# A fourth Strassen weight combination in a tile of its own, and four activation combinations moved between the products

## The chip, the cores and the metric

The kernel runs on one core of one Trainium2 chip. The metric is the device time of one execution in microseconds. A time is the median of several runs. The profile is one execution of its own, so it has its own time, and its trace has a span: the first to the last recorded instruction.

## The reference, cut to what matters

The model is one inference step through two layers. Each layer holds two SwiGLU feed-forward blocks ("FFN") around a token mixer, all in 32-bit floats. There are 640 token rows: 512 latent and 128 of context. Only the FFN matters here:

```python
def swiglu(h, w_in, w_out):
    a, b = jnp.split(h @ w_in, 2, axis=-1)
    return (jax.nn.silu(a) * b) @ w_out

n = rmsnorm(x, ng[0]) * (1.0 + mod[..., 1, :]) + mod[..., 0, :]
x = x + 0.5 * mod[..., 2, :] * swiglu(n, lp['w_ffn_in'][0], lp['w_ffn_out'][0])
```

`w_in` is 1024 x 5632 (two halves of 2816 columns, the a half and the b half) and `w_out` is 2816 x 1024.

## The kernel before

**Tiles and products.** Activations lie transposed: 128 channels by 320 tokens, two token halves (h = 0 and 1), eight blocks of channels. A product of 32-bit floats is made as three matmuls with a high and a low part each: hi x hi, hi x lo, lo x hi. So every weight block that arrives (a "raw" tile `wr_*`, 512 KB) is split: ScalarE (ACT) casts the high part (`wh_*`), VectorE (DVE) subtracts it from the raw block to get the low part (`wl_*`). The weights are read once; TensorE (PE) is the engine that has most to do.

**Quads.** Three of the four FFNs are "fast": layer 0's second (about 1262 to 1700 us of the trace), layer 1's first (1727 to 2150) and layer 1's second (2850 to 3300). In them 18 of the 22 column blocks of `w_in` are computed with a Strassen-Winograd 2x2 scheme, class `Quad`, 54 quads in all. A quad takes one a block `fa` and one b block `fb`, and needs seven products (`p` 1 to 7) of 12 matmuls each in place of the eight that plain blocks need. Its weights come in four groups:

- group 0: `wh_fa`, `wl_fa`, the a block itself (products 1 and 2). With it GpSimd (POOL) makes the combinations, four instructions that stand one behind the other: L86 `ws` (S1), L87 `ws` (S2), L88 S3 in place in `fb`, L89 S4 in place in the upper half of `fa`.
- group 1: `wh_g<-wr_fb`, `wl_g<-wr_fb` (products 7 and 4), split out of `fb` after L88.
- group 2: `wh_g<-ws`, `wl_g<-ws` (products 6 and 5).
- group 3: `whg` (L97) and `wlg` (L98), half a tile, split out of S4 (product 3).

PE takes the products of quad after quad in the order 1, 7, 3 of the quad before, 6, 4 of the quad before, 2, 5. Products 1, 6 and 5 accumulate in one PSUM tile `qx`, which ACT copies out after each of them (`qs`, L124) before PE may add the next; products 7 and 4 go to `qw`, product 2 to `qy`. After product 3 come ACT and DVE instructions that make the FFN's hidden values: `sa` (L1465, L1468), and their split `fhi`, `flo` (L903, L904).

**Queues and pools.** Each engine runs its own instruction list in order. SyncE (SP) issues the weight loads in order (L1235). Raw tiles come from a pool of three buffers (`RAW = 3`): a quad's two blocks and one of the next. `emit` walks the list of steps and asks for a load as soon as enough raw blocks count as "gone": a tuple says for each of a quad's four groups how many are let go with it, (0, 0, 1, 1) before. A load that reuses a buffer waits for the last instruction that reads or writes the block that was in it.

**Activation combinations.** Product 4 needs a combined activation, made by `combine4` in four chunks (k = 0 to 3): DVE adds `e` (L1404), POOL adds `t` (L1403) and subtracts `t - e` (L1405), ACT casts `nhi` and DVE makes `nlo` (L903, L904 through `put`). Tile `e` has tag "nt" with two buffers, which it shares with the copies `qs` of products 1 and 5; `t` has tag "tt", two buffers. An FFN is done in four parts of its hidden columns (5, 5, 6 and 6 blocks), q = 0 to 3. In part 0 the first four column blocks are plain (`pa`, `pb`), since the combinations are made meanwhile, so part 0 has a single quad; its products come in the order 1, 7, 6, 2, 5, 3, 4. `rest` issues all four `combine4` before that quad.

Of the kernel before, what the change touches and what calls it, by code (L numbers as in the profile page):

```python
# [10 lines left out]
F32 = mybir.dt.float32  # L11
# [6 lines left out]
P = 128  # L18
# [46 lines left out]
class Quad:  # L65
# [12 lines left out]
    def split(self, g, raws):  # L78
        b, sub, add = self.b, ALU.subtract, ALU.add
        fa, fb = raws  # L80
        T = b.nc.gpsimd.tensor_tensor
        if g == 0:
            self.s = b.tq.tile([P, 8, P], F32, tag="ws", name=f"ws_{self.name}", bufs=1)
            r = b.split(self.blocks[0], fa)
            s2, s1 = self.s[:, 0:4], self.s[:, 4:8]
            T(s1, fb[:, 0:4], fb[:, 4:8], add)  # L86
            T(s2, s1, fa[:, 0:4], sub)  # L87
            T(fb[:, 0:4], fa[:, 0:4], fb[:, 0:4], sub)  # L88
            T(fa[:, 4:8], fa[:, 4:8], s2, sub)  # L89
            return r  # L90
        if g == 1:
            return b.split((None, 8, f"g2{self.name}"), fb)
        if g == 2:
            return b.split((None, 8, f"g3{self.name}"), self.s)
        hi = b.tq.tile([P, 4, P], F32R, tag="whi4", name=f"whg4{self.name}", bufs=1)
        lo = b.tq.tile([P, 4, P], F32R, tag="wlo4", name=f"wlg4{self.name}", bufs=1)
        b.nc.scalar.copy(hi, fa[:, 4:8])  # L97
        b.nc.vector.tensor_tensor(lo, fa[:, 4:8], hi.bitcast(F32), sub)  # L98
        return hi, lo

    def product(self, out, w, p, first):
# [54 lines left out]
class Build:  # L156
# [1101 lines left out]
    def emit(self, steps):  # L1258


        last, order, seen = {}, [], set()
        for i, st in enumerate(steps):
            if not callable(st):
                last[id(st[0])] = i
                if id(st[0]) not in seen:
                    seen.add(id(st[0]))
                    order.append(st[0])

        blocks, splits = [], []
        done = {id(u): [] for u in order}  # L1270
        for u in order:
            n0 = len(blocks)
            if isinstance(u, Quad):
                blocks += u.blocks
                for g in range(4):
                    splits.append((u, lambda u=u, g=g, n0=n0: u.split(g, raws[n0 : n0 + 2]), n0 + 2, (0, 0, 1, 1)[g], g == 3))
            else:
                for i, tl in enumerate(u[0]):
                    blocks.append(tl)
                    splits.append((u, lambda tl=tl, n=n0 + i: self.split(tl, raws[n]), n0 + i + 1, 1, False))  # L1280
        raws = []
        cnt = {"split": 0, "gone": 0, "live": 0, "fourth": 0}

        def load():
            raws.append(self.load(blocks[len(raws)]))

        def room():
            return cnt["fourth"] < 1 if splits[cnt["split"]][4] else cnt["live"] < SPL

        def split():  # L1290
            u, f, need, gone, fourth = splits[cnt["split"]]
            while len(raws) < need:
                load()
            with self.ahead(WS):
                done[id(u)].append(f())
            cnt["split"] += 1
            cnt["gone"] += gone
            cnt["fourth" if fourth else "live"] += 1

        def fill():  # L1300
            while True:
                while len(raws) < len(blocks) and len(raws) - cnt["gone"] < RAW:
                    load()
                if cnt["split"] == len(splits) or not room():
                    break
                split()

        fill()
        for i, st in enumerate(steps):
            if callable(st):  # L1310
                st()
                continue
            u, h = st
            quad = isinstance(u, Quad)
            while len(done[id(u)]) < (u.NEED[h] if quad else len(u[0])):
                assert room()
                split()
            if quad:
                u.run(done[id(u)], h)
                cnt["live"] -= u.FREE[h]  # L1320
                cnt["fourth"] -= h == 3
                if u.FREE[h] or h == 3:
                    fill()
                if h in (6, 5):
                    self.late()
                    self.tick()
                continue
            with self.ahead(EV):
                u[1](done[id(u)], h)
            self.late()  # L1330
            self.tick()
            if last[id(u)] == i:
                cnt["live"] -= len(u[0])
                fill()
# [80 lines left out]
    def ffn(self, l, i, pre=None, post=None, fast=False, late=None):  # L1415
# [4 lines left out]
        steps = []  # L1420
        for q, nf in enumerate(FPARTS):
            j0 = sum(FPARTS[:q])
            end = q == len(FPARTS) - 1
            f = {}
# [13 lines left out]
            ins, outs, quads = [], [], []  # L1438
# [53 lines left out]
            if fast and q == 0:  # L1492

                def rest():
                    while self.deferred:
                        self.late()
                    for k in range(4):
                        self.combine4(k, f"{l}{i}")

                steps.append(rest)  # L1500
            steps += Quad.steps(quads)
            if end and late:
                steps.append(late)
            steps += self.edges(outs, 0, 4 if end else 0, post=post if end else None)
# [240 lines left out]
```

## Time and profile before

| | us |
|---|---|
| median of 3 runs | 3338.36 (3335.77 to 3343.9) |
| the profiled execution | 3330.81 |
| its span in the trace | 3329.0 |
| PE busy in it | 3213.5 (97%) |
| DVE busy | 2124.0 (64%) |
| ACT busy | 1291.7 (39%) |
| POOL busy | 494.8 (15%) |

The mean granted TensorE clock of the profiled execution is 0.989 of full speed. Times in the trace are counted from the span's start. A busy PE is a PE with a matmul in flight: it can be busy and still lose time between two matmuls, so the idle time of PE and of its weight loads (PEld) are both read below.

### The profile page before, as it was taken

To read this page: it belongs to the slowest core of one execution; us is meant where nothing else is said; L and a number is where in the kernel's file an instruction comes from. 1 tells how busy PE (TensorE), PEld (TensorE's weight loads), DVE (VectorE), ACT (ScalarE), POOL (GpSimd) and SP (SyncE) were. 2 spreads that over 40 slices of the span, in tenths; PEclk is the share of its full clock that TensorE was granted. 3 is DMA by queue.
4 is the path that set the end of the run, shared out by engine and by line. 5 is a ranking of instruction groups with operands and counts; after the bars stand their busy time and mean duration, and the time that the engine had idled before them with its cause. 6 is when DMAs were issued, how large, how long until landed. Compare 5 with 4: busy or idle time off the path is not lost.

```text
span 3329.0 us, 56455 instructions
## 1 busy us (share of the span) xinstructions
PE 3213.5 (97%) x22321; PEld 3028.1 (91%) x22321; DVE 2124.0 (64%) x4543; ACT 1291.7 (39%) x2596; POOL 494.8 (15%) x418
## 2 busy tenths in 40 slices
PE   6999999989999999999999999998999999999998
PEld 5887999879989999899998889997998999999998
DVE  5656574796686348566667556668758734856665
ACT  4233233554453224234343323445545423433432
POOL 0000000120000013222312312312000000322231
PEclk8999999989999999999999999998999999999999
DMA  6666433433313324522224553234331243122222
GB/s 220 185 192 205 129 117 109 131 113 98 92 50 115 92 73 120 173 83 83 75 80 145 175 160 89 67 117 122 98 90 52 63 138 88 53 75 79 87 70 76
DMA packets 493995, 364.55 MB, mean 110 GB/s; under 512 B 22466, under 2 KB 468260, under 8 KB 490916
## 3 DMA queue, kind: packets, MB, share of 16 engines
q1 hardware_dynamic: 463284, 311.33, 31.4%
q10 hardware_dynamic: 30448, 49.62, 4.3%
q8 instruction: 176, 2.88, 0.4%
q14 instruction: 87, 0.71, 0.1%
HBM read 327.33 MB, written 33.55 MB: 108 GB/s over the span
## 4 chain that ended last, share of the span: by engine, by line
PE 75%; DVE 15%; issue 4%; ACT 3%; DMA 3%; POOL 0%; DVEq 0%; ACTq 0%; SPq 0%; POOLq 0%
PE po L1254 6%; PE po L1255 6%; PE po L1256 6%; PE mg L1254 3%; PE mg L1256 3%; PE mg L1255 3%; PE qx L108 2%; PE qx L109 2%; PE pa L1254 2%; PE mps L284 2%; PE qx L110 2%; PE pa L1255 2%; PE pa L1256 2%; PE pb L1255 2%; PE pb L1254 2%
## 5 line engine op out<-in xcount | busy, mean ns | idle before, releaser
L1254 PE MATMUL po<-fhi,wh_fo 128*128 128x320 f32 x1408 | 444.6, 316 | 0.2
L1255 PE MATMUL po<-flo,wh_fo 128*128 128x320 f32 x1408 | 435.7, 310 | 0.0
L1256 PE MATMUL po<-fhi,wl_fo 128*128 128x320 f32 x1408 | 435.3, 310 | 0.0
L1254 PEld LDWEIGHTS po<-fhi,wh_fo 128*128 128x128 f32 x1408 | 263.9, 188 | 36.0 <-issue 31.5
L360 POOL TENSOR_TENSOR acc<-acc,sq 128x320 f32<-128x320 f32 x72 | 77.3, 1074 | 1339.2 <-ACT sq L359 1339.0
L1255 PEld LDWEIGHTS po<-flo,wh_fo 128*128 128x128 f32 x1408 | 264.5, 188 | 3.2 <-issue 2.7
L1256 PEld LDWEIGHTS po<-fhi,wl_fo 128*128 128x128 f32 x1408 | 264.2, 188 | 2.3 <-issue 2.3
L1254 PE MATMUL mg<-nhi,wh_wg 128*128 128x320 f32 x768 | 239.3, 312 | 0.0
L1256 PE MATMUL mg<-nhi,wl_wg 128*128 128x320 f32 x768 | 238.1, 310 | 0.0
L1255 PE MATMUL mg<-nlo,wh_wg 128*128 128x320 f32 x768 | 237.7, 310 | 0.0
L1244 ACT CAST wh_fo<-wr_fo 128x640 fp32r<-128x640 f32 (+1 forms) x128 | 100.0, 781 | 236.5 <-PE po L1255 183.9
L1510 DVE SCALAR_TENSOR_TENSOR xT0b<-po,mod,xT0b 128x64 f32<-128x64 f32 (+1 forms) x256 | 86.9, 379 | 149.6 <-PE po L1256 149.3
L1254 PE MATMUL pa<-nhi,wh_fa 128*128 128x320 f32 x544 | 173.2, 319 | 1.0 <-ACT nhi L422 1.0
L1255 PE MATMUL pa<-nlo,wh_fa 128*128 128x320 f32 x544 | 168.1, 312 | 1.2 <-DVE nlo L423 1.1
L1256 PE MATMUL pa<-nhi,wl_fa 128*128 128x320 f32 x544 | 168.5, 310 | 0.0
L1256 PE MATMUL pb<-nhi,wl_fb 128*128 128x320 f32 x544 | 168.4, 310 | 0.0
L1255 PE MATMUL pb<-nlo,wh_fb 128*128 128x320 f32 x544 | 168.3, 309 | 0.0
L1254 PE MATMUL pb<-nhi,wh_fb 128*128 128x320 f32 x544 | 168.2, 309 | 0.0
L86 POOL TENSOR_TENSOR ws<-wr_fb 128x512 f32<-128x512 f32 x54 | 73.9, 1368 | 624.5 <-DMA wr_fb<-in_w_ffn_in_dram 529.2
L1244 ACT CAST wh_fa<-wr_fa 128x1024 fp32r<-128x1024 f32 x88 | 92.5, 1051 | 149.0 <-PE po L1255 93.3
L1254 PEld LDWEIGHTS mg<-nhi,wh_wg 128*128 128x128 f32 x768 | 144.5, 188 | 2.3 <-issue 1.9
L1255 PEld LDWEIGHTS mg<-nlo,wh_wg 128*128 128x128 f32 x768 | 144.3, 188 | 0.5 <-issue 0.5
(531 smaller groups left out, 9818.7 us busy)
## 6 DMA issues: line engine op xcount, KB each, us to landing
wmod<-in_w_mod_dram SPq DMA_DIRECT2D x144, 512.0 KB, 4.1
wr_fa<-in_w_ffn_in_dram SPq DMA_DIRECT2D x88, 512.0 KB, 4.0
wr_fb<-in_w_ffn_in_dram SPq DMA_DIRECT2D x88, 512.0 KB, 4.5
wr_fo<-in_w_ffn_out_dram SPq DMA_DIRECT2D x64, 384.0 KB, 3.4
wr_wg<-in_w_in_dram SPq DMA_DIRECT2D x48, 512.0 KB, 4.4
wr_fo<-in_w_ffn_out_dram SPq DMA_DIRECT2D x64, 320.0 KB, 3.5
pqd<-s5pq ACTq DMA_DIRECT2D x16, 1024.0 KB, 7.6
wr_wb<-in_w_branch_dram SPq DMA_DIRECT2D x48, 256.0 KB, 2.8
```

Source lines behind the costliest of these rows:

```text
L86: T(s1, fb[:, 0:4], fb[:, 4:8], add)
L108: mm(out, a, ahi(k), start=(first and k == 0), stop=False, skip_group_check=True)
L109: mm(out, a, alo(k), start=False, stop=False, skip_group_check=True)
L110: mm(out, c, ahi(k), start=False, stop=(k == 3), skip_group_check=True)
L284: nc.tensor.matmul(pm[32 * j : 32 * j + 32, :256], self.sc[:, k, :], w[:, j * 256 : (j + 1) * 256], start=(k == 0), stop=(k == KD - 1),)
L360: (nc.vector if k == KD - 1 else nc.gpsimd).tensor_tensor(self.acc[:, h], self.acc[:, h], sq, ALU.add)
L1244: nc.scalar.copy(hi[:, :kk], raw[:, :kk])
L1254: nc.tensor.matmul(out, hi[:, k], ahi(k), start=(k == 0), stop=False)
L1255: nc.tensor.matmul(out, hi[:, k], alo(k), start=False, stop=False)
L1256: nc.tensor.matmul(out, lo[:, k], ahi(k), start=False, stop=(k == kk - 1))
L1510: self.nc.vector.scalar_tensor_tensor(x, po[:, sl], gate[:, n, g : g + 1], x, ALU.mult, ALU.add)
```

## The change

Three edits. S4 (L89) goes into a tile of its own, `ws4`, with one buffer, and `whg` and `wlg` are split out of that tile; nothing writes into `fa` any more. The tuple of raw blocks let go becomes (1, 1, 0, 0). And `combine4` leaves `rest`: its four chunks are put as steps of their own between the products of part 0's single quad: 1, chunk 0, 7, chunk 1, 6, chunk 2, 2, chunk 3, 5, 3, 4.

```diff
@@ -86,7 +86,8 @@
             T(s1, fb[:, 0:4], fb[:, 4:8], add)
             T(s2, s1, fa[:, 0:4], sub)
             T(fb[:, 0:4], fa[:, 0:4], fb[:, 0:4], sub)
-            T(fa[:, 4:8], fa[:, 4:8], s2, sub)
+            self.s4 = b.tq.tile([P, 4, P], F32, tag="ws4", name=f"ws4{self.name}", bufs=1)
+            T(self.s4, fa[:, 4:8], s2, sub)
             return r
@@ -94,8 +95,8 @@
         hi = b.tq.tile([P, 4, P], F32R, tag="whi4", name=f"whg4{self.name}", bufs=1)
         lo = b.tq.tile([P, 4, P], F32R, tag="wlo4", name=f"wlg4{self.name}", bufs=1)
-        b.nc.scalar.copy(hi, fa[:, 4:8])
-        b.nc.vector.tensor_tensor(lo, fa[:, 4:8], hi.bitcast(F32), sub)
+        b.nc.scalar.copy(hi, self.s4)
+        b.nc.vector.tensor_tensor(lo, self.s4, hi.bitcast(F32), sub)
         return hi, lo
@@ -1273,7 +1274,7 @@
                 for g in range(4):
-                    splits.append((u, lambda u=u, g=g, n0=n0: u.split(g, raws[n0 : n0 + 2]), n0 + 2, (0, 0, 1, 1)[g], g == 3))
+                    splits.append((u, lambda u=u, g=g, n0=n0: u.split(g, raws[n0 : n0 + 2]), n0 + 2, (1, 1, 0, 0)[g], g == 3))
@@ -1494,11 +1495,14 @@
                 def rest():
                     while self.deferred:
                         self.late()
-                    for k in range(4):
-                        self.combine4(k, f"{l}{i}")
 
                 steps.append(rest)
-            steps += Quad.steps(quads)
+            st = Quad.steps(quads)
+            if fast and q == 0:
+
+                for k in range(4):
+                    st.insert(2 * k + 1, lambda k=k: self.combine4(k, f"{l}{i}"))
+            steps += st
```

In the changed program lines behind L89 have moved by one: S4 is L90, `whg` and `wlg` are L98 and L99, `e` is L1405. The order of PE's instructions does not change at all.

What waits for what does change. Before, the load of the next quad's `fb` takes over a buffer that is free when DVE has made `wl_g<-wr_fb` of the current quad, and the load of the `fa` behind it one that is free at `wlg`, the last reader of the raw `fa`. After, the next `fb` takes the current `fa`'s buffer, which is free when DVE has made `wl_fa` and POOL has made S4; the `fa` behind it takes the current `fb`'s, free at `wl_g<-wr_fb`.

POOL's list in two quads of the second part, before (L86 to L89 are S1, S2, S3, S4; `wr_fa`, `wr_fb` the raw blocks):

```order
L86 TENSOR_TENSOR ws_14816<-wr_fb_14731 128x512
L87 TENSOR_TENSOR ws_14816<-ws_14816,wr_fa_14589 128x512
L88 TENSOR_TENSOR wr_fb_14731<-wr_fa_14589,wr_fb_14731 128x512
L89 TENSOR_TENSOR wr_fa_14589<-wr_fa_14589,ws_14816 128x512
L86 TENSOR_TENSOR ws_14949<-wr_fb_14864 128x512
```

and POOL's list at the same place with the change:

```order
L86 TENSOR_TENSOR ws_14819<-wr_fb_14651 128x512
L87 TENSOR_TENSOR ws_14819<-ws_14819,wr_fa_14537 128x512
L88 TENSOR_TENSOR wr_fb_14651<-wr_fa_14537,wr_fb_14651 128x512
L90 TENSOR_TENSOR ws_14827<-wr_fa_14537,ws_14819 128x512
L86 TENSOR_TENSOR ws_14953<-wr_fb_14829 128x512
```

The order is the same. But L89 overwrote the `fa` block that DVE's `wl_fa` still had to read, and so had to wait for it; L90 writes `ws4` (shown as `ws_14827`) and has nothing of DVE's to wait for but the `wlg` of the quad before.

ACT's list at the single quad of part 0 of the first fast FFN, before (`nhi` are the casts of the four chunks, the two `qs` the copies of `qx` after products 1 and 6):

```order
L1244 CAST wh_g_14007<-ws_13872 128x1024
L1451 ACTIVATE sa_13996<-pa_13946 128x320
L903 CAST nhi<-t_14025 128x320
L903 CAST nhi<-t_14032 128x320
L903 CAST nhi<-t_14039 128x320
L1244 CAST wh_fo_14019<-wr_fo_13712 128x640
L1453 CAST fhi_13328<-sa_13996 128x320
L903 CAST nhi<-t_14046 128x320
L124 COPY qs_14066<-qx_14053 128x320
L124 COPY qs_14093<-qx_14053 128x320
```

and with the change:

```order
L1245 CAST wh_g_14012<-ws_13872 128x1024
L1452 ACTIVATE sa_14001<-pa_13951 128x320
L1245 CAST wh_fo_14020<-wr_fo_13712 128x640
L1454 CAST fhi_13328<-sa_14001 128x320
L125 COPY qs_14039<-qx_14026 128x320
L904 CAST nhi<-t_14041 128x320
L904 CAST nhi<-t_14061 128x320
L904 CAST nhi<-t_14088 128x320
L904 CAST nhi<-t_14116 128x320
L125 COPY qs_14080<-qx_14026 128x320
```

The copy after product 1 has moved ahead of all four casts; the copy after product 6 stands right behind them.

DVE's list ahead of that quad, before (`wl_fa` and `wl_g` are the quad's own weights, `sa` and `flo` still belong to the plain blocks):

```order
L1404 TENSOR_TENSOR e_14026<-thi_13326,tlo_13327 128x320
L1404 TENSOR_TENSOR e_14033<-thi_13326,tlo_13327 128x320
L1245 TENSOR_TENSOR wl_fa_13874<-wr_fa_13621,wh_fa_13873 128x1024
L1404 TENSOR_TENSOR e_14040<-thi_13326,tlo_13327 128x320
L1404 TENSOR_TENSOR e_14047<-thi_13326,tlo_13327 128x320
L1452 TENSOR_TENSOR sa_13843<-sa_13843,pb_13794 128x320
L98 TENSOR_TENSOR wlg_14014<-wr_fa_13621,whg_14013 128x512
L1245 TENSOR_TENSOR wl_g_13882<-wr_fb_13706,wh_g_13881 128x1024
```

and the end of the same stretch with the change:

```order
L1246 TENSOR_TENSOR wl_g_14013<-ws_13872,wh_g_14012 128x1024
L1453 TENSOR_TENSOR sa_14001<-sa_14001,pb_13952 128x320
L1246 TENSOR_TENSOR wl_fo_14021<-wr_fo_13712,wh_fo_14020 128x640
L1455 TENSOR_TENSOR flo_13329<-sa_14001,fhi_13328 128x320
L1405 TENSOR_TENSOR e_14042<-thi_13326,tlo_13327 128x320
L1405 TENSOR_TENSOR e_14062<-thi_13326,tlo_13327 128x320
L905 TENSOR_TENSOR nlo<-t_14041,nhi 128x320
L1405 TENSOR_TENSOR e_14089<-thi_13326,tlo_13327 128x320
L905 TENSOR_TENSOR nlo<-t_14061,nhi 128x320
L1405 TENSOR_TENSOR e_14117<-thi_13326,tlo_13327 128x320
```

The four `e` have moved from ahead of the quad's weights to behind the last plain block's `flo`, each `nlo` between them. The second `e` now finds one of the two "nt" buffers held by the copy after product 1, so from there each `e` waits until POOL has used the one before.

## Rows read from the trace of the kernel before

**Rows 1.** The page, busy time of each engine (us, share of the span, instructions).

```profile
PE 3213.5 (97%) x22321; PEld 3028.1 (91%) x22321; DVE 2124.0 (64%) x4543; ACT 1291.7 (39%) x2596; POOL 494.8 (15%) x418
```

**Rows 2.** Waits: engine, tile, line, what it waited for; us in total, times, longest.

```profile
POOL ws L86 <- DMA wr_fb<-in_w_ffn_in_dram: 529.2, 43, 40.8
POOL wr_fa L89 <- DVE wl_fa L1245: 91.8, 35, 3.8
...
PEld qw L110 <- DVE wl_g L1245: 24.6, 30, 0.9
...
PEld qx L108 <- ACT qs L124: 10.0, 11, 5.8
```

**Rows 3.** Tile qx, what ended the idle time before it (us, times).

```profile
  DVE wl_fa L1245: 5.6, 17
```

**Rows 4.** Timeline of PE's weight loads, product 7 of one quad.

```profile
1422.40 0.19 PEld L110 LDWEIGHTS qw<-thi,wl_g 128*128 128x128 f32 x1 [0.87 <-DVE wl_g L1245]
```

**Rows 5.** Chain that ended last, 1410 to 1437 us (start, us, what).

```profile
1412.09 0.16 PE qx L109
1412.33 0.63 ACT whg L97
...
1420.43 1.93 DVE wl_g L1245
...
1425.62 0.16 PE qx L109
```

**Rows 6.** Timeline of POOL, the same quad.

```profile
1412.80 1.29 POOL L86 TENSOR_TENSOR ws<-wr_fb 128x512 f32<-128x512 f32 x1 [5.05 <-DMA wr_fb<-in_w_ffn_in_dram]
1414.17 1.63 POOL L87 TENSOR_TENSOR ws<-ws,wr_fa 128x512 f32<-128x512 f32 x1
1415.75 1.55 POOL L88 TENSOR_TENSOR wr_fb<-wr_fa,wr_fb 128x512 f32<-128x512 f32 x1
1419.85 1.41 POOL L89 TENSOR_TENSOR wr_fa<-wr_fa,ws 128x512 f32<-128x512 f32 x1 [2.55 <-DVE wl_fa L1245]
```

**Rows 7.** Timeline of DVE, the same quad.

```profile
1412.98 1.66 DVE L98 TENSOR_TENSOR wlg<-wr_fa,whg 128x512 fp32r<-128x512 f32 x1 [2.61 <-ACT whg L97]
1414.57 1.58 DVE L1468 TENSOR_TENSOR sa<-sa,c 128x320 f32<-128x320 f32 x1
1416.67 0.97 DVE L904 TENSOR_TENSOR flo<-sa,fhi 128x320 fp32r<-128x320 f32 x1 [0.53 <-ACT fhi L903]
...
1418.08 0.49 DVE L1468 TENSOR_TENSOR c<-c,c 128x320 f32<-128x320 f32 x1
1418.49 1.22 DVE L1245 TENSOR_TENSOR wl_fa<-wr_fa,wh_fa 128x1024 fp32r<-128x1024 f32 x1
...
1420.43 1.92 DVE L1245 TENSOR_TENSOR wl_g<-wr_fb,wh_g 128x1024 fp32r<-128x1024 f32 x1
```

**Rows 8.** Timeline of SP, the quad's `fb` load; under it the page's issues.

```profile
1408.86 0.37 SPq L1235 DMA_DIRECT2D wr_fb<-in_w_ffn_in_dram  x1
...
wr_fb<-in_w_ffn_in_dram SPq DMA_DIRECT2D x88, 512.0 KB, 4.5
```

**Rows 9.** Timeline of DVE ahead of the last fast FFN's single quad.

```profile
2911.67 0.68 DVE L98 TENSOR_TENSOR wlg<-wr_fa,whg 128x512 fp32r<-128x512 f32 x1
```

**Rows 10.** Timeline of PE, first matmul of product 6, third and second fast FFN.

```profile
2920.66 0.63 PE L108 MATMUL qx<-thi,wh_g 128*128 128x320 f32 x1 [5.49 <-ACT qs L124]
...
1799.13 0.63 PE L108 MATMUL qx<-thi,wh_g 128*128 128x320 f32 x1 [2.12 <-ACT qs L124]
```

**Rows 11.** Windows: length, busy us (instructions) of PE, PEld, DVE, ACT, POOL, granted clock, DMA.

```profile
2920.60:2926.00 5.40, 5.34 (x22) 5.35 (x23) 0.67 (x2) 0.43 (x2) 0.00 (x0) 0.56 0.20 61
```

**Rows 12.** Timeline of ACT and POOL at that quad, and of ACT in the first fast FFN.

```profile
2920.18 0.42 ACT L124 COPY qs<-qx 128x320 f32<-128x320 f32 x1
...
2917.04 0.86 POOL L1405 TENSOR_TENSOR t<-t,e 128x320 f32<-128x320 f32 x1
...
1326.60 0.42 ACT L124 COPY qs<-qx 128x320 f32<-128x320 f32 x1
```

## The prediction

> **What bounds the kernel.** Start with the page's busy times: PE has a matmul in flight in 97% of the span [rows 1], so only time lost between matmuls is to be had. The waits view, read for PE's weight loads, names two places where the fast FFNs lose it [rows 2]: loads for `qw` wait for DVE's `wl_g` 24.6 us in 30 waits, and loads for `qx` for ACT's copy `qs` 10.0 us in 11, one of them 5.8. The tile's own view adds 5.6 us in 17 waits of `qx` for `wl_fa` [rows 3]. A weight load is normally issued while an earlier matmul runs, so its idle time is what PE loses; the first number, of product 7's third matmul, is 0.87 in one quad [rows 4]. POOL's waits, 529.2 us for the `fb` block and 91.8 us in 35 waits for `wl_fa` [rows 2], are not PE's time, but they say when the combinations are made.
>
> Next the chain, over one quad of the second part [rows 5]: product 3 ends, ACT casts `whg`, then DVE goes through `wlg`, `sa`, `flo`, two `c`, `wl_fa`, `flo`, `c` to `wl_g`, and product 7 waits for that. From matmul to matmul of product 3 the quad takes 1425.62 - 1412.09 = 13.53 us; 84 matmuls at 0.147 (1.76 for a product's 12) are 12.3, so it loses 1.2.
>
> Then DVE beside POOL. Three operations of DVE take more than twice what the same shape takes elsewhere: `wlg` 1.66 against 0.68 [rows 7, 9], `sa` 1.58 against 0.49 for `c` of the same line, `flo` 0.97 against 0.49; and `wl_g` 1.92 against 1.22 for `wl_fa` of the same size [rows 7]. Each overlaps a POOL operation [rows 6], and each POOL operation that begins beside one is longer too (1.63 and 1.55 against 1.29). The ends alternate: POOL to 1414.09, DVE to 1414.64, POOL to 1415.80, DVE to 1416.15, POOL to 1417.30, DVE to 1417.64. From 1414.64 to 1415.80, POOL alone moved on: a POOL operation costs the DVE chain 1.15 us if it falls wholly on it. The four excesses sum to 0.98 + 1.09 + 0.48 + 0.70 = 3.25 us.
>
> **Part 1: the steady quads (S4's own tile, and raw blocks let go earlier).** Count from product 3's end, 1412.22. PE then needs 48 matmuls (products 6, 4, 2, 5) before product 1, whose third matmul's load reads `wl_fa` one matmul on: 7.04 + 0.15 = 7.19. It needs `wl_g` one product later: 8.95. `wl_fa` ended at 1418.49 + 1.22 - 1412.22 = 7.49, `wl_g` at 10.13 [rows 7]; 0.30 and then 0.88 late, the sum of the loss. Without contention `wl_g` would come at 10.13 - 3.25 = 6.88, so the chain can bear 2.07 us of POOL.
>
> Where does POOL go? The `fb` load was issued at 1408.86, -3.36 [rows 8], right behind `wl_g` of the quad before, and POOL began S1 at +0.58, 3.94 later. After, it is issued behind `wl_fa` of the quad before, since S4 ends sooner: 7.2 after the last product 3, which is 12.3 before the next, so at about -5.1. With 3.94 of transfer POOL starts at -1.2; with the page's median of 4.5 [rows 8] at -0.6. DVE's chain begins only when `whg` is cast, at +0.76 [rows 7]. S1 (1.29) is then done before it. S2, S3 and S4 follow without a pause, since S4 no longer waits for `wl_fa`; the alternation gives DVE one turn behind each. With a start at -1.2: S2 to 1.3 costs `wlg` 0.5, S3 costs `sa` 1.1, S4 costs the rest of the wait for `fhi` and 0.5 of `flo`: 2.1, and `wl_g` is in time. With a start at -0.6: 0.9 + 1.1 + 0.6 = 2.6, 0.5 late. A late `wl_g` lengthens the quad and so gives the load more time, which halves the lateness. I take 0.25 us for each of the 30 stalled quads, and no `wl_fa` stalls. The stalls are 24.6 + 5.6 = 30.2 us; 30 x 0.25 = 7.5 stays: **22.7 us gained**. Bounds: 30.2 if all goes, 12 at 0.6 a quad.
>
> The `fa` load behind it now is let go at `wl_g<-wr_fb`, about 1 us after `fb`'s rather than 5.8 us after; the two transfers overlap, the reason for taking the later landing. SP's list has nothing else between them but modulation weights, whose turn comes sooner, not later. `ws4` costs no instruction: S4 has the same operands but one. It must wait for the `wlg` of the quad before, some 10 us earlier.
>
> The Trainium skill, "SBUF — State Buffer", section "Who interferes with whom", calls the port pair that GpSimd and VectorE share the only contended one, and an exclusive lock, not a split of bandwidth. The alternating ends agree. That rule speaks against moving S4 up beside the other three, since it frees no port time; by it the whole gain must come from S1 being made while DVE is idle.
>
> **Part 2: part 0's single quad in each fast FFN (`combine4` moved).** Before, the copy after product 1 stands behind four `nhi` casts that wait for POOL. In the third fast FFN it ran at 2920.18 [rows 12] and product 6 began at 2920.66, 5.49 us of idle PE [rows 10], and the 22 matmuls that followed took 5.40 us at a granted clock of 0.56 [rows 11], between the levels 1.2 and 2.4 GHz, where 22 x 0.147 = 3.2 would do: 5.65 + 2.2 = 7.8 us. In the second it was 2.12 us of idle [rows 10], about 2.3 + 1.3 in the same proportion. In the first the copy came at 1326.60 [rows 12], in time. Together 11.4.
>
> After, the copy is behind `fhi` only, whose `sa` needs the last plain block's `pb`; product 1 follows that on PE, so the copy is ready at the end of product 1 and product 6 doesn't wait. But the copy after product 6 now stands behind the four casts. From `e0`, which DVE can begin about when product 1 ends, the chain is: `e` 0.49, `t - e` 0.86 [rows 12], again for the second, `t` and `t - e` for the third (its buffer comes free with the first `nlo`), and again: some 7 us to the last cast, plus the copy. Product 5 needs it two products after product 6's start, 5.3 us after product 1's end: it waits about 2 us in the third FFN, as much in the second, and in the first, where all was in time, it loses 0.8 (the modulation work there hides part). Third: 5.65 of gain at a full clock, 4.3 if the new wait brings the lower clock for as long as the second FFN's did; second 3.1 or 2; first -0.8. **Gain 7 us**, bounds 3 and 11.4.
>
> **Sum.** 23 + 7 = 30. The profiled execution's 3330.8 becomes 3300.8. The median of the runs is 7.6 above that execution, so 3338.4 - 30 = 3308.
>
> **The rivals.** (a) *A third to a half of the steady gain stays out*: the two overlapped transfers bring `fb` at 0 rather than -1, S1 falls on `wlg`, and 0.6 us a quad remain: 12 + 4 = 16 less, 3322. For it: a landing of 4.5 is the median and some take longer. Against: `fb` is issued ahead of `fa`.
> (b) *No change to speak of*: with a landing from about +0.2 on, POOL's four operations fall on the chain as before, only S4 takes `flo` and not `wl_g`; part 2 alone gives 3 to 7: 3331 to 3335. It takes a transfer of 5.3 us for 3.94. That `fb` is not issued earlier, because S4 ends after `wl_fa`, would do the same; S4 ends near 5, `wl_fa` at 7.2, so it doesn't decide.
> (c) *Slower*: POOL holds the lock through S1 to S4 without giving DVE its turn. Then `wlg` begins at -0.6 + 4 x 1.2 = 4.2 in place of 0.76, 3.4 late where 2.07 is allowed: 1.3 a quad in place of 1.2, and also in the quads that now lose nothing because modulation matmuls give them time, 20 or so of the 54: 51 x 1.35 = 69 against 30.2, less part 2's 7: about 32 us slower, 3370. It decides from a POOL start of -1.9 on. The Trainium skill's section named above says that the lock is held for an instruction and does not say who is next. The trace's alternation, three times in this quad, speaks against it; before, POOL's next operation was ready there too.
>
> **Chances.** As forecast (gain 22 to 42): 0.58. (a) gain 10 to 22: 0.24. (b) within 10: 0.13. (c) 0.05. A measurement tells 0.3%, 10 us. So faster 0.82, same 0.13, slower 0.05. The likeliest case's own range is 3297 to 3316; the range over the cases is 3295 to 3330: its low end is nearly all of 30.2 + 11.4, its high end part 2's gain alone.
>
> **What would show it.** Right: POOL's L86 starts before product 3 ends, L90 begins right behind L88, `wl_g<-wr_fb` takes 1.22, the waits of `qw` for `wl_g` fall from 24.6 to under 10, those of `qx` for `wl_fa` go, and the quads are under 12.7 us apart. In part 0's quad product 6 follows product 7 without a gap and product 5 waits about 2 us for `qs`. Wrong: the DMA wait of L86 ends after product 3, or `wlg`, `sa` and `flo` grow by more than before, or product 5's wait is above 4 us with a long stretch at the lower clock.

## The result and the profile after

The changed kernel takes 3309.19 us (median of 4 runs) against 3337.07 us before (4 runs), a ratio of 0.9912 with a 95% interval of 0.9899 to 0.9925. One run of the four, 4462.04 us at a granted clock of 0.642, is counted in that median and left out of the ratio. The forecast was 3308.

The profiled execution of the changed kernel took 3309.53 us, 21.3 less than the one before (3330.81). Set each matmul beside the same matmul of the trace before, and see where the distance changes: it is +4.4 us by 1306 us, before the first quad's products (+0.9 by 105 us and +4.1 by 210, a stretch in which modulation weights arrive and nothing was changed), and -20.9 at the end. From the first fast FFN on, then, 25.3 us were gained in this pair of traces. Where they came from is in the same comparison and in the views below.

First the waits of PE's weight loads, the longest groups (engine, tile, line, what it waited for; us in total, times, longest), which answer to [rows 2]:

```profile
PEld po L1255 <- issue: 31.9, 77, 0.8
PEld mps L285 <- issue: 23.1, 119, 0.3
PEld mps L285 <- DMA wmod<-in_w_mod_dram: 22.6, 21, 3.8
...
PEld qx L109 <- ACT qs L125: 9.8, 11, 3.8
```

The 24.6 us for `wl_g` are not smaller, they are gone: the list has no such row, nor one for `wl_fa`. The wait for the copy `qs` stands where it stood, 9.8 us against 10.0.

Now the timeline of POOL in the second part (start, us, what, idle time before it and its releaser), against [rows 6]:

```profile
1420.69 1.30 POOL L86 TENSOR_TENSOR ws<-wr_fb 128x512 f32<-128x512 f32 x1 [6.58 <-DVE c L132]
1422.07 1.29 POOL L87 TENSOR_TENSOR ws<-ws,wr_fa 128x512 f32<-128x512 f32 x1
1423.32 1.29 POOL L88 TENSOR_TENSOR wr_fb<-wr_fa,wr_fb 128x512 f32<-128x512 f32 x1
1425.31 1.41 POOL L90 TENSOR_TENSOR ws<-wr_fa,ws 128x512 f32<-128x512 f32 x1 [0.69 <-DVE wlg L99]
```

and of DVE in the same quad, against [rows 7]:

```profile
1423.92 1.24 DVE L99 TENSOR_TENSOR wlg<-ws,whg 128x512 fp32r<-128x512 f32 x1 [3.24 <-ACT whg L98]
1425.08 0.48 DVE L1469 TENSOR_TENSOR sa<-sa,c 128x320 f32<-128x320 f32 x1
1426.09 0.97 DVE L905 TENSOR_TENSOR flo<-sa,fhi 128x320 fp32r<-128x320 f32 x1 [0.53 <-ACT fhi L904]
...
1427.91 1.22 DVE L1246 TENSOR_TENSOR wl_fa<-wr_fa,wh_fa 128x1024 fp32r<-128x1024 f32 x1
...
1429.85 1.22 DVE L1246 TENSOR_TENSOR wl_g<-wr_fb,wh_g 128x1024 fp32r<-128x1024 f32 x1
```

Product 3 ends here at 1423.16. S1 starts 2.5 us before that (0.6 after it in [rows 6]), and S1, S2 and the first 0.6 us of S3 run while DVE waits for `whg`. Of the four excesses of DVE, 3.25 us before, two smaller ones are left: `wlg` 1.24 against 0.68 and `flo` 0.97 against 0.49, 1.04 us together. `sa`, 1.58 before, takes 0.48: it began while POOL was waiting for `wlg`, before S4. `wl_g` ends at 1431.07, 7.91 after product 3, where PE needs it at 8.95. That is 1.0 us to spare, and a quad takes 12.3 us.

The `fb` load (timeline of SP) is issued as soon as `wl_fa` of the quad before ends, 1416.72:

```profile
1416.78 0.37 SPq L1236 DMA_DIRECT2D wr_fb<-in_w_ffn_in_dram  x1
1418.68 0.37 SPq L1236 DMA_DIRECT2D wr_fa<-in_w_ffn_in_dram  x1
```

S1 begins 3.9 us later, at 1420.69. The row of POOL names DVE's `c` (L132) as what released it, because that ended last before S1, but `c` reads and writes neither `ws` nor `wr_fb`. The old `ws` was free when DVE had made `wl_g` from it, at 1420.28 (timeline of DVE):

```profile
1419.05 1.23 DVE L1246 TENSOR_TENSOR wl_g<-ws,wh_g 128x1024 fp32r<-128x1024 f32 x1 [0.40 <-ACT wh_g L1245]
```

The semaphore updates in the trace put the landing of the transfer at 1420.53, 3.75 us after its issue. So S1 waited last for the transfer, which came 0.25 us after `ws` was free. The waits of POOL in the whole program, against [rows 2]:

```profile
POOL ws L86 <- DMA wr_fb<-in_w_ffn_in_dram: 389.4, 18, 47.1
...
POOL ws L86 <- DVE wl_g L1246: 186.7, 18, 17.4
...
POOL ws L86 <- DVE c L132: 111.9, 17, 7.7
...
POOL ws L90 <- DVE wlg L99: 23.2, 32, 1.2
```

The row for `c` is to be read as the transfer too: in all 17 the landing lies 0.16 us before S1, as it does where the transfer is named in a steady quad. Counted so, S1 waits last for the transfer 35 times now, against 45 before (43 so named and two put down to `sa`). It still waits for it; what has changed is when it lands. Over the quads that follow one another the median start of S1 is 2.4 us before product 3's end, against 0.6 after it. The last row is a new wait that has taken the place of the one for `wl_fa` (91.8 us in 35).

Then the single quad of part 0. Timeline of PE, the first matmul of product 5 in the three fast FFNs, against product 6 in [rows 10]:

```profile
1337.93 0.41 PE L109 MATMUL qx<-thi,wh_g 128*128 128x320 f32 x1 [1.92 <-ACT qs L125]
...
1804.24 0.42 PE L109 MATMUL qx<-thi,wh_g 128*128 128x320 f32 x1 [1.95 <-ACT qs L125]
...
2915.65 0.42 PE L109 MATMUL qx<-thi,wh_g 128*128 128x320 f32 x1 [3.51 <-ACT qs L125]
```

Product 6 waits nowhere, as forecast; product 5 waits instead, and now in all three. The timeline of ACT before the third shows the queue, against [rows 12]:

```profile
2908.46 0.46 ACT L904 CAST nhi<-t 128x320 fp32r<-128x320 f32 x1 [1.08 <-POOL t L1406]
2910.22 0.46 ACT L904 CAST nhi<-t 128x320 fp32r<-128x320 f32 x1 [1.30 <-POOL t L1406]
2912.53 0.46 ACT L904 CAST nhi<-t 128x320 fp32r<-128x320 f32 x1 [1.85 <-POOL t L1406]
2914.81 0.46 ACT L904 CAST nhi<-t 128x320 fp32r<-128x320 f32 x1 [1.82 <-POOL t L1406]
2915.17 0.42 ACT L125 COPY qs<-qx 128x320 f32<-128x320 f32 x1
```

Product 6 ended at 2910.2; its copy began 5.0 us later, behind the last cast. And the window behind the wait (length, busy us and instructions of PE, PEld, DVE, ACT, POOL, granted clock, DMA) has the lower clock again, as in [rows 11]:

```profile
2915.60:2919.00 3.40, 3.35 (x14) 3.35 (x15) 1.42 (x3) 1.55 (x3) 0.00 (x0) 0.60 0.14 41
```

Measured by the distance of equal matmuls, moving `combine4` cost 3.5 us in the first fast FFN, and gained 1.6 in the second and 2.9 in the third: 1 us in all. The steady quads gave about 30, and most now follow each other at 12.3 us, 13.1 to 13.6 before. About 4.7 us went to matmuls on modulation weights that waited for their transfers, above all at 1384 us, and about 1 is spread over the mixer.

### The profile page after: what moved, and what is told of

It reads as the page before. It is cut to its first block, busy times and chain, and to the rows that moved or that the text cites. A ratio compares the mean times of both kernels' runs of the same rounds, so it can differ in the third digit from the quotient of the medians.

```text
span 3307.7 us, 56423 instructions
## 1 busy us (share of the span) xinstructions
PE 3206.4 (97%) x22321; PEld 3030.2 (92%) x22321; DVE 2064.9 (62%) x4543; ACT 1299.1 (39%) x2596; POOL 482.6 (15%) x418
## 4 chain that ended last, share of the span: by engine, by line
PE 82%; DVE 10%; DMA 3%; issue 2%; ACT 2%; POOL 1%; SPq 0%; DVEq 0%; POOLq 0%; ACTq 0%
PE po L1255 6%; PE po L1256 5%; PE po L1257 5%; PE qx L109 4%; PE qx L110 4%; PE qx L111 4%; PE mg L1255 3%; PE mg L1257 3%; PE mg L1256 3%; PE pa L1255 2%; PE pa L1256 2%; PE pa L1257 2%; PE pb L1256 2%; PE pb L1255 2%; PE pb L1257 2%
## 5 line engine op out<-in xcount | busy, mean ns | idle before, releaser
L86 POOL TENSOR_TENSOR ws<-wr_fb 128x512 f32<-128x512 f32 x54 | 71.4, 1322 | 688.0 <-DMA wr_fb<-in_w_ffn_in_dram 389.4
L99 DVE TENSOR_TENSOR wlg<-ws,whg 128x512 fp32r<-128x512 f32 x54 | 55.8, 1033 | 169.9 <-ACT whg L98 169.9
```

What stands on the lines that cost most here:

```text
L99: b.nc.vector.tensor_tensor(lo, self.s4, hi.bitcast(F32), sub)
```

## The experiments

Ratios are to the kernel before, run on the same chip, with 95% intervals.

**1. S4's tile without the move of `combine4`.** The changed kernel with this undone:

```diff
-            st = Quad.steps(quads)
-            if fast and q == 0:
-                for k in range(4):
-                    st.insert(2 * k + 1, lambda k=k: self.combine4(k, f"{l}{i}"))
-            steps += st
+            steps += Quad.steps(quads)
```

and the two lines back in `rest`.

> The changed kernel with combine4 back in rest, so that only S4's own tile and the tuple are changed. Theory 1 (from the trace after the change): the steady quads gave all 30.2 us of stalls, moving combine4 about 1 us net, and some 4 us went to modulation weights that came late; so this lands near 3310, with no wait of qw for wl_g, product 6 waiting again for the copy in the second and third fast FFN (about 2 and 5.5 us) and product 5 waiting nowhere. Rival (the prediction's sizes): moving combine4 is worth 7 us, and this lands near 3316.

Measured: 3308.31 us, ratio 0.992 (0.9907 to 0.9932), the same as the whole change. Its trace has no wait for `wl_g` or `wl_fa`, and one row for the copy, with product 6 in the third fast FFN as the longest:

```profile
PEld qx L109 <- ACT qs L125: 9.3, 11, 5.3
```

**2. The move of `combine4` alone.** The kernel before with the other half of the diff.

> The kernel before with only combine4 moved between the products. Theory 1: about 1 us faster than before, near 3336, with the 30 waits for wl_g as before. Rival (the prediction's size): 7 us faster, near 3330.

Measured: 3336.33 us, ratio 1.0004 (0.9996 to 1.0013): no gain. Waits of the weight loads:

```profile
PEld qw L110 <- DVE wl_g L1245: 22.7, 30, 0.9
...
PEld qx L108 <- ACT qs L124: 9.8, 11, 3.8
```

The wait for the copy has its old size at its new place, and the quads stall as before. The two halves of the change are one that gives everything and one that gives nothing that the times can tell (a gain of 1 us lies just inside the interval); the size of 7 us for the second is refuted.

**3. S4's tile, but the block let go late.** The changed kernel with a reader of the raw `fa` behind `wl_g`:

```diff
-            return b.split((None, 8, f"g2{self.name}"), fb)
+            r = b.split((None, 8, f"g2{self.name}"), fb)
+            z = b.tq.tile([P, 1], F32, tag="zz", name=f"zz{self.name}", bufs=1)
+            b.nc.vector.tensor_tensor(z, r[1][:, 0, 0:1].bitcast(F32), fa[:, 0, 0:1], add)
+            return r
```

> The changed kernel plus one small DVE instruction per quad that reads the raw fa block behind wl_g of group 1, so that fb's load is let go as late as before the change, while S4 keeps its own tile and does not wait for wl_fa. Theory 1: what counts is when the fb load is let go, since that sets how many POOL operations fall on DVE's chain; the stalls of 0.9 us a quad come back, 20 to 30 us, 3330 to 3338. Rival: what counts is that S4 no longer waits for wl_fa and no longer meets wl_g; then most of the gain stays, 3310 to 3318.

Measured: 3338.05 us, ratio 1.0004 (0.9995 to 1.0013). The whole gain is gone. The added instruction takes 0.16 us, in all quads together 8.5 us of an engine that is busy 62% of the span in the changed kernel. The timeline of POOL shows S1 waiting for its transfer past product 3's end again, which was at 1431.5 here, and S4 close behind S3 (the median start of S1 is 0.8 us after product 3's end, against 0.6 in the kernel before):

```profile
1432.78 1.34 POOL L86 TENSOR_TENSOR ws<-wr_fb 128x512 f32<-128x512 f32 x1 [7.68 <-DMA wr_fb<-in_w_ffn_in_dram]
...
1437.09 1.54 POOL L90 TENSOR_TENSOR ws<-wr_fa,ws 128x512 f32<-128x512 f32 x1
```

The timeline of DVE shows which operation S4 meets now, and the waits of the weight loads what that costs:

```profile
1437.40 2.32 DVE L1249 TENSOR_TENSOR wl_fa<-wr_fa,wh_fa 128x1024 fp32r<-128x1024 f32 x1
```

```profile
PEld qx L114 <- DVE wl_fa L1249: 18.5, 19, 1.0
...
PEld qw L114 <- DVE wl_g L1249: 6.1, 22, 0.8
```

24.6 us of stalls, most of them a product earlier. So S4's freedom from `wl_fa` alone gives nothing; what counts is when the `fb` block is let go. With that late, S4 without its wait only moves from `wl_g` to `wl_fa`: 2.32 against 1.22. An early `fb` with an S4 that still waits was not run: a load that takes the `fa` buffer has to wait for S4 as well.

**4. `combine4` placed in two halves.** Chunks 0 and 1 in `rest`, chunks 2 and 3 later than in the change:

```diff
+                    self.combine4(0, f"{l}{i}")
+                    self.combine4(1, f"{l}{i}")
...
-                for k in range(4):
-                    st.insert(2 * k + 1, lambda k=k: self.combine4(k, f"{l}{i}"))
+                for at, k in ((4, 2), (6, 3)):
+                    st.insert(at, lambda k=k: self.combine4(k, f"{l}{i}"))
```

> The changed kernel with chunks 0 and 1 of combine4 back in rest and chunks 2 and 3 put behind product 6 and 2, so that neither copy of qx stands behind four casts. Theory 1: product 5's stalls and the half clock after them go (3.5, 2.1 and 4.3 us in the three fast FFNs) and product 6 doesn't wait: 8 to 10 us faster than the changed kernel, 3299 to 3302. Rival: chunk 2's cast still waits for POOL ahead of the copy after product 6, and half of it stays, 3304 to 3307.

Measured: 3295.11 us, ratio 0.988 (0.9865 to 0.9895), the interval apart from that of the change: better by 0.3 to 0.4%, and more than expected. Waits of the weight loads for the copy, whole program:

```profile
PEld qx L109 <- ACT qs L125: 1.9, 9, 0.3
```

The timeline of ACT in the third fast FFN shows why: one cast ahead of the copy after product 6, one behind the copy after product 5.

```profile
2901.96 0.46 ACT L904 CAST nhi<-t 128x320 fp32r<-128x320 f32 x1 [2.06 <-POOL t L1406]
2902.33 0.42 ACT L125 COPY qs<-qx 128x320 f32<-128x320 f32 x1
...
2906.17 0.42 ACT L125 COPY qs<-qx 128x320 f32<-128x320 f32 x1
2906.77 0.46 ACT L904 CAST nhi<-t 128x320 fp32r<-128x320 f32 x1 [0.19 <-POOL t L1406]
```

Against the changed kernel's trace, 3.7, 2.2 and 5.0 us go at the three single quads (a wait, and in the first and third the slow matmuls behind it), and 2.9 at the modulation weights near 1384 us, though SP's loads stand in the same order in both traces. Those 2.9 were no part of the expectation.

**5. The tuple put back.** The changed kernel with `(0, 0, 1, 1)[g]`.

> The changed kernel with the tuple put back to (0, 0, 1, 1), S4's own tile and the moved combine4 kept. Theory 1: the buffer that a load takes over, and what that waits for, follow from the last reader of the block in it, which S4's own tile alone has changed; the tuple does nothing, 3309 as the changed kernel, no waits for wl_g. Rival (as the change is described): the tuple lets the raw blocks go earlier, and without it the loads are as late as before, 3330 or more.

Measured: 3310.3 us, ratio 0.992 (0.9907 to 0.9934). In the traces the instructions of DVE, ACT and POOL and the loads of SP stand in the changed kernel's order, row by row. The tuple does nothing.

**6 and 7. More work for POOL.** One and two more subtractions of S2's size between S3 and S4, their results unused:

```diff
+            self.x0 = b.tq.tile([P, 4, P], F32, tag="wsx", name=f"wsx0{self.name}", bufs=1)
+            T(self.x0, s1, fa[:, 0:4], sub)
```

> The changed kernel with one more POOL subtraction of S2's size between S3 and S4 of each quad (its result is not used). Theory 1: in the changed kernel wl_g comes about 1.0 us before product 7 needs it, and a POOL operation costs DVE's chain at most 1.15 us, here about 0.8 since part of it meets idle DVE time; so the quads lose nothing or 0.1 to 0.2 us each, 3309 to 3314. Rival: POOL's operations cost the chain nothing once the fb block is early: 3309, and the next kernel too.

> The same with two more POOL subtractions in each quad. Theory 1: the second one and S4 fall wholly on DVE's chain, about 2 us more than in the changed kernel where 1.0 is to spare, so some 30 to 35 quads lose 0.8 to 1.2 us each again: 3333 to 3350, with waits for wl_fa or wl_g as in the kernel before. Rival: 3309 to 3314.

Measured: 3325.74 us (ratio 0.9965, 0.9953 to 0.9977) and 3353.8 us (1.0059, 1.0047 to 1.0072): 16.6 and 44.6 us above the changed kernel. One operation cost more than expected. DVE's timeline of the first of them says why:

```profile
1423.44 1.57 DVE L1471 TENSOR_TENSOR sa<-sa,c 128x320 f32<-128x320 f32 x1
1425.54 0.98 DVE L907 TENSOR_TENSOR flo<-sa,fhi 128x320 fp32r<-128x320 f32 x1 [0.53 <-ACT fhi L906]
...
1426.95 1.07 DVE L1471 TENSOR_TENSOR c<-c,c 128x320 f32<-128x320 f32 x1
```

and the timeline of POOL which operation each of them met (L90 is the added one, L92 is S4):

```profile
1422.93 1.73 POOL L88 TENSOR_TENSOR wr_fb<-wr_fa,wr_fb 128x512 f32<-128x512 f32 x1
1424.63 1.54 POOL L90 TENSOR_TENSOR wsx<-ws,wr_fa 128x512 f32<-128x512 f32 x1
1426.13 1.54 POOL L92 TENSOR_TENSOR ws<-wr_fa,ws 128x512 f32<-128x512 f32 x1
```

In the changed kernel the three take 0.48, 0.97 and 0.49. S3 meets `sa` now (1.09 longer), the added operation takes S4's place on `flo`, and S4 is pushed back onto `c` (0.58 longer). That is 1.7 us more, less 0.3 by which `wlg` is shorter in this quad, where 1.0 was to spare. S3 has come to `sa` because S1 starts only 1.5 us before product 3's end here, 2.5 in the changed kernel's quad: `wl_fa` is later by then, and the load goes out behind it. The expectation counted one operation on a chain that was otherwise as before. Waits of the weight loads with one and with two:

```profile
PEld qx L113 <- DVE wl_fa L1248: 8.4, 19, 1.0
...
PEld qw L113 <- DVE wl_g L1248: 3.7, 22, 0.2
```

```profile
PEld qx L115 <- DVE wl_fa L1250: 37.1, 30, 2.1
...
PEld qw L115 <- DVE wl_g L1250: 5.1, 30, 0.2
```

**8. Modulation loads ahead again.** Experiment 4 with the late reader of experiment 3 in the 9 quads made while modulation weights stream in (`if b.sides:`).

> The split placement of combine4 (its run was the fastest so far) with the late release of the fa block in those 9 quads alone that are made while modulation weights stream in, which puts the modulation loads ahead of the fb loads again in SP's list. Theory 1: the matmuls on modulation weights no longer wait 0.5 to 2.4 us for their weights, and these quads have time enough for the late fb block: 2 to 4 us faster than the split placement, 3291 to 3294. Rival: the waits for modulation weights differ from run to run whatever SP's order: same as the split placement, 3295, or slower by stalls of wl_fa.

Measured: 3294.92 us, ratio 0.9875 (0.9862 to 0.9889), as experiment 4. The wait of the modulation matmuls is somewhat shorter, 18.4 us in 18 waits against 21.9 in 23:

```profile
PEld mps L289 <- DMA wmod<-in_w_mod_dram: 18.4, 18, 2.3
```

The order of the loads is then worth nothing that the times can tell. That the waits at 1384 us in the changed kernel's trace came from SP's list (a modulation load that stood behind an `fb` load, itself waiting, was issued about 1 us late) was only read from the trace. The kernel before and experiment 2, which keeps its list but for four lines, have no such gap over 0.5 us from matmul to matmul between 1255 and 2000 us, and the changed kernel and experiments 1, 3, 4 and 5 have two to four each, of 0.5 to 2.6. But experiment 8 has two of 0.8 to 0.9 with the loads ahead again. And with one and the same list the wait at 1384 us is 2.35 us from matmul to matmul in the changed kernel, 1.24 in experiment 1 and 1.00 in experiment 4. What sets them stays open.

## Why the prediction was right, and where it was not

**What bounds it, and the mechanism of part 1: right.** PE lost its time at the two places named. In the steady quads the stalls came from POOL's operations on DVE's chain, and what moved them off it was the earlier `fb` load: experiment 3 takes that away and leaves S4 its tile, and all is lost; experiment 1 keeps the tile without the move of `combine4`, and all is kept. Experiments 6 and 7 put operations back on the chain, and the stalls return. Rival (c), POOL holding the lock through all four, did not come. Experiment 6 shows it where POOL's next operation had nothing to wait for: S3 ended at 1424.66, `sa` at 1425.01, and only then, at 1426.17, the added operation.

**The term of part 1 was too small: 22.7 us forecast, 30.2 measured.** Three steps of it were off. The load was counted from `wl_fa` at 7.2 us after product 3, the time by which PE needs it, though with the contention gone `wl_fa` ends at 1416.72, 5.9 after that quad's product 3. The load goes out that much earlier; with a transfer of 4.5 us it would land at 1421.3, still 1.9 before product 3 ends. The transfer was taken at 4.5 us because of the `fa` load behind it, and took 3.75 here. And "S2, S3 and S4 follow without a pause", with `wlg` of the quad before "some 10 us earlier", was wrong: S4 waits for just that `wlg`, 0.69 us here and 32 times in all, because `ws4` has one buffer and group 3 of a quad is split while POOL makes the next. It cost nothing: `sa`, to which the sum charged 1.1, began in that pause and took 0.48.

**The term of part 2 was wrong: 7 us forecast, about 1 in the traces, none in the times (experiment 2).** The new place of the wait was right, its size was not. In the first fast FFN the loss of 0.8 was a wait of 1.92, and slow matmuls behind it (a granted clock of 0.71 over the next 3.4 us). The second waited 1.95 as forecast, but gained 1.6 and not 2 to 3.1. The third FFN was forecast to wait 2 and waited 3.51: the chain from the first `e` at 2906.92 to the copy at 2915.17 takes 8.3 us, not 7. The third and fourth `e` run beside POOL's `t` and take 1.15 and 1.13 us, not 0.49. The contention that part 1 counts with care was left out of part 2. What the wait costs is also more than its length: at a granted clock of 0.60, 14 matmuls took 3.4 us where 2.1 would do.

**A cost was left out, or was chance.** "Modulation weights, whose turn comes sooner" was not so in the built order: several `fb` loads moved one place ahead of one of them. The trace lost about 4.7 us on such waits; experiment 8 found no time in the order.

So the sum of 30 was 22.7 + 7, and what happened is 30 + 1 less some 5 for the modulation waits. In the profiled pair 4.1 more went in the first 210 us, before any changed instruction. The medians are 27.9 us apart and the profiled pair 21.3: the execution that was profiled before is faster than each of its four timed runs. The forecast of 3308 against 3309 owes part of its closeness to these errors offsetting each other.

**The tuple.** The prediction gave it the earlier release, together with S4's tile. Experiment 5 shows that it is the tile alone.

## What to carry to other kernels

When a stall is found in a chain of one engine, look for what runs beside it and when that was released: here a buffer freed 3 us sooner (6.4 us before product 3's end, against 3.4), by a combination that no longer wrote into the block, was worth the whole gain, and the wait that was removed in name alone nothing. Before moving an instruction out of another's way in an in-order queue, list what stands behind it at the new place: the four casts blocked one copy as well as the other, and with two ahead and two late neither waited more than 0.3 us. And count a chain's operations at their contended length wherever the other engine is one link of the same chain.

## What the runs showed of the hardware

The recorded times of a DVE operation with two operands in SBUF and of a POOL operation overlap, but in the quads read their ends take turns: a DVE operation that met one ended after it, by 0.1 us less than its own length alone. In experiment 6 S3 ends at 1424.66 and `sa`, 0.48 alone, at 1425.01; in experiment 3 S4 ends at 1438.63 and `wl_fa`, 1.22 alone, at 1439.72. A POOL operation that falls wholly on one put about 1.1 us on it (`sa` 0.48 and 1.57; `wl_fa` 1.22 and 2.32). The Trainium skill, "SBUF — State Buffer", section "Who interferes with whom", calls the port pair that GpSimd and VectorE share an exclusive lock. These rows agree, and experiments 6 and 7 put a time on it: 1 us to spare in a quad absorbs less than one such operation, and two cost 44.6 us over the program.

After PE had waited 5.49 us in the third fast FFN before the change, and 3.51 us after it, the granted clock of the next 5.4 and 3.4 us was 0.56 and 0.60, between the levels of 1.2 and 2.4 GHz. The length of the wait did not settle it: after two waits of nearly the same length in the changed kernel, 1.92 us in the first fast FFN and 1.95 in the second, it was 0.71 and 1.00 over the next 3.4 us.
